# Where the fourth operand sum of layer 0's MLP is subtracted on VectorE

## The chip, the core and the metric

The kernel runs on one core of one Trainium2 chip. TensorE (PE) multiplies, with weight loads (PEld) that overlap its matmuls; VectorE (DVE), ScalarE (ACT) and GpSimd (POOL) do elementwise work; SyncE (SP) and ACT issue most DMAs. The metric is the time of one execution on the device, in microseconds (us).

## The reference

A two-layer encoder over two sequences (`x_prompt` and `x_sample`, each 512 tokens of width 1024, float32). Layer 0 mixes by a grouped Fourier transform, layer 1 by attention; each is followed by a squared-ReLU MLP of width 4096. The change lies in the MLP of layer 0:

```python
def rms_norm(x, g):
    x32 = x.astype(jnp.float32)
    y = x32 * lax.rsqrt(jnp.mean(x32 * x32, axis=-1, keepdims=True) + EPS)
    return (y * g.astype(jnp.float32)).astype(x.dtype)

def sq_relu_mlp(h, w_up, w_down):
    a = jnp.maximum(h @ w_up, 0)
    return (a * a) @ w_down

def trunk(x, ...):
    for i in range(DEPTH):
        j = i // N_MIXERS
        if i % N_MIXERS == 0:
            x = x + fourier_mix(rms_norm(x, fourier_norm[j]), fourier_w_out[j])
        else:
            x = x + gqa_attention(...)
        x = x + sq_relu_mlp(rms_norm(x, mlp_norm[i]), mlp_w_up[i], mlp_w_down[i])
    return rms_norm(x, final_norm)
```

## The kernel before, in words

**Precision.** A float32 product is made of three matmuls. Each operand is split into a high half (float32r, a cast on ACT, L82) and a low half (operand minus high half, a subtraction on DVE, L83); `product` (L863 on, matmul at L869) does high times high, high times low and low times high, accumulated in one PSUM bank. Over four blocks of depth, that is 12 matmuls of 128x128 by 128x512.

**The MLP's product in seven.** The up-projection of both sequences together is a 2x2 block product, and the kernel does it with seven block products instead of eight. The blocks are: sequence 0 or 1 on one side, and the lower or upper half of the model width on the other. The operands on the activations' side are two blocks of sequence 0 ("b11", "b21"), one block of sequence 1 ("b22") and four sums ("t1" to "t4"). With f[0] and f[1] the normed activations of the two sequences, c in (0, 1) a half of each operand:

- t1 = f[1, c] - f[0, c] (L266)
- t2 = f[1, 2+c] - t1 (L267)
- t3 = f[1, 2+c] - f[1, c] (L271), in place of f[1, c]
- t4 = f[0, 2+c] - t2 (L278), in place of f[0, 2+c]

Each half is a 128x1024 tile. `put` splits it into two new tiles of 128x1024 (high and low). All such tiles, the activations and the outputs of a pair come from one pool of 38 buffers ("u" in the trace, `slot` in the code); raw weights come from a pool of 5 ("raw"), split weights from one of 4 ("w").

**Order of the work around the change.** The class `Blocks` makes the operands. In layer 0 the generator `second_sums` makes those that need sequence 1, a step at each `yield`: for each half the norm of two blocks (L208), t1, t2 and t2's split; then t3 and its split; t1's split; t4 and its split; b22's split. `first_product` runs it while PE does the products that need sequence 0 alone. A pair p (16 in layer 0) is two tiles of 128 hidden units. `Pair.first` is the product with b11, copied out of PSUM by ACT at L903; `Pair.second` adds the product with b21 in the same bank, and ACT makes its squared ReLU (L884, L885). Pairs 0 to 7 do both of these ahead of the sums. In the loop over p = 0 to 7, PE does pair p's first product and pair p-1's second, the next pair's row weights are loaded and split, and then, from p = 3 on, three steps of `second_sums` are taken. Steps 1 to 3 (norms, t1 and t2 of c = 0) fall in p = 3, those of c = 1 in p = 4, t3 and the first t1 split in p = 5, the second t1 split and both t4 in p = 6, and b22 in p = 7. The sums of pair 0's own weights are made in between (`sums_13` at L918 and L919, `sum_2` at L922, `sum_4` at L930).

After the loop, `Pair.rest` does the products with t2, t3, t1, t4 and b22 for each pair, adds them up on DVE (L947 to L981), and makes, in the same turn, the weight sums of the next pair. Pairs 8 to 15 do their first and second products within it.

**Who sets the order.** The framework's scheduler orders each engine's instructions, by their place in the source and by when it takes their inputs to be ready; in the blocks under `manual_schedule` the named engines keep an order written out by hand. In the loop over p = 0 to 7 that holds for PE's products alone; the steps of `second_sums`, DVE, ACT and SP are the scheduler's. A buffer is given out again when the last reader of its old tile has run.

```python
            if p > 3 - whole:
                for _ in range(3 - 2 * l):
                    next(todo, None)
```

Of the kernel before, what the change touches and what calls it, by code (L numbers as in the profile page):

```python
# [40 lines left out]
def trunk_kernel(ctx, tc, x_in, xt_in, y_out, dcos, dsin, feat, rope, gfour, gcol, grow, gfin,  # L41
                 w_four, w_nyq, w_qkv, w_o, w_up, w_row2, w_row4, w_sum2, w_sum4, w_down):
    nc = tc.nc
# [17 lines left out]
    def slot(shape, dt):  # L61
        return act.tile(shape, dt, tag="u4", name=nm("u"))
# [122 lines left out]
    class Blocks:  # L185
# [70 lines left out]
        def second_sums(self):  # L256

            f, t1, t2 = self.f, [], []
            for c in range(2):
                self.norm(1, c)  # L260
                yield
                self.norm(1, 2 + c)
                yield
                t1.append(slot([P, 2, 512], F32))
                t2.append(slot([P, 2, 512], F32))
                nc.vector.tensor_sub(t1[c], f[1, c], f[0, c])  # L266
                nc.vector.tensor_sub(t2[c], f[1, 2 + c], t1[c])  # L267
                self.put("t2", t2[c])
                yield
            for c in range(2):  # L270
                nc.vector.tensor_sub(f[1, c], f[1, 2 + c], f[1, c])  # L271
                self.put("t3", f[1, c])
                yield
            for c in range(2):
                self.put("t1", t1[c])
                yield
            for c in range(2):
                nc.vector.tensor_sub(f[0, 2 + c], f[0, 2 + c], t2[c])  # L278
                self.put("t4", f[0, 2 + c])
                yield  # L280
            for c in range(2, 4):
                self.put("b22", f[1, c])
                yield
# [1672 lines left out]
```

## Time and profile before

| | us |
|---|---|
| median of 3 runs | 1694.37 |
| lowest, highest | 1693.82, 1695.23 |
| the profiled execution | 1695.11 |
| its span | 1693.3 |
| PE busy in the span | 1681.2 |
| DVE, ACT busy | 1228.0, 854.3 |
| mean granted TensorE clock | 0.999 |

The profile is of one execution. A row of a timeline gives the start in us from the span's start, the length in us, the engine, the line in the kernel, the operation, what is written and read (by the program's names without numbers) with its shape, and how many of them follow each other; in brackets stands how long the engine had been idle, and who ended that. A row of waits gives who waited for whom, the total in us, how often, and the longest. A row of a stretch gives its length, and busy us with the number of instructions for PE, PEld, DVE, ACT and POOL in turn, then the granted clock, the DMAs' busy share and GB/s. Matmuls are pipelined and their ends are modelled, so PE's busy time contains the overlap of neighbours.

### The profile page before, as it was taken

How to read it: one execution, taken by the hardware profiler on the slowest of the kernel's cores; microseconds unless marked ns; L12 is line 12 of the kernel's file. 1: busy time of each engine (PE TensorE's matmuls, PEld its weight loads, DVE VectorE, ACT ScalarE, POOL GpSimd, SP SyncE). 2: the span in 40 equal slices, each digit the busy share in tenths (PEclk: the TensorE clock that was granted, in tenths of full speed). 3: DMA queues.
4: the chain of work that ended last, by engine and by line, in shares of the span. 5: the costliest groups of instructions: out<-in, count | busy, mean ns of one | idle time of the engine just before them, and what ended most of it. 6: DMA issues, size and time to landing. Idle time of an engine off the chain costs nothing. (4 is left out here: it accounts for less than half of the span.)

```text
span 1693.3 us, 21857 instructions
## 1 busy us (share of the span) xinstructions
PE 1681.2 (99%) x7845; PEld 1395.0 (82%) x7845; DVE 1228.0 (73%) x1808; ACT 854.3 (50%) x1489; POOL 334.9 (20%) x304
## 2 busy tenths in 40 slices
PE   9999999999999999999999999999999999999998
PEld 7987888888888888888888888888888888888887
DVE  8778776557887879876588744687655479787864
ACT  7566444446243434457787714654444544344334
POOL 1321443221000000132344303014422200000002
PEclk9999999999999999999999999999999999999999
DMA  9643555449554644610000213335544686455322
GB/s 340 167 137 126 198 187 180 156 168 388 178 209 140 224 139 172 223 50 33 26 26 1 100 61 126 110 120 193 180 143 156 224 303 236 159 210 183 133 75 100
DMA packets 103679, 265.81 MB, mean 157 GB/s; under 512 B 10177, under 2 KB 10177, under 8 KB 103570
## 3 DMA queue, kind: packets, MB, share of 16 engines
q1 hardware_dynamic: 87266, 232.43, 39.2%
q10 hardware_dynamic: 14400, 26.22, 4.1%
q0 software_dynamic: 1904, 5.77, 1.7%
q8 instruction: 61, 1.00, 0.2%
q14 instruction: 48, 0.39, 0.1%
HBM read 189.40 MB, written 73.92 MB: 156 GB/s over the span
## 5 line engine op out<-in xcount | busy, mean ns | idle before, releaser
L869 PE MATMUL ps<-u,w 128*128 128x512 f32 x4656 | 1065.4, 389 | 1.4 <-ACT u L903 0.7
L869 PEld LDWEIGHTS ps<-u,w 128*128 128x128 f32 x4656 | 872.7, 188 | 185.6 <-ACT u L903 2.7
L82 ACT CAST w<-raw 128x1024 fp32r<-128x1024 f32 (+1 forms) x224 | 217.5, 981 | 445.1 <-PE ps L869 244.5
L83 DVE TENSOR_TENSOR w<-raw,w 128x1024 fp32r<-128x1024 f32 (+1 forms) x224 | 255.6, 1144 | 60.8 <-ACT w L82 60.3
L156 POOL TENSOR_TENSOR t<-t,t 128x512 f32<-128x512 f32 (+1 forms) x56 | 77.7, 1388 | 738.3 <-ACT t L154 682.2
L82 ACT CAST u<-u 128x1024 fp32r<-128x1024 f32 (+1 forms) x131 | 131.3, 1044 | 76.0 <-PE ps L869 47.2
L83 DVE TENSOR_TENSOR u<-u,u 128x1024 fp32r<-128x1024 f32 (+1 forms) x131 | 155.3, 1211 | 19.3 <-ACT u L82 18.6
L77 PE MATMUL ps<-u,u 128*128 128x512 f32 (+2 forms) x388 | 150.2, 388 | 0.4 <-DVE u L83 0.4
L1141 DVE TENSOR_TENSOR u<-ps,u 128x512 f32<-128x512 f32 x160 | 109.4, 686 | 51.2 <-PE ps L869 48.9
L78 PE MATMUL ps<-u,u 128*128 128x512 f32 (+2 forms) x388 | 144.4, 372 | 0.4 <-DVE u L83 0.3
L79 PE MATMUL ps<-u,u 128*128 128x512 f32 (+2 forms) x388 | 144.4, 372 | 0.0
L869 PE MATMUL ps<-u,u 128*128 128x512 f32 x576 | 137.8, 390 | 0.2 <-DVE u L1141 0.2
L869 PEld LDWEIGHTS ps<-u,u 128*128 128x128 f32 x576 | 107.9, 188 | 23.8 <-DVE u L1141 0.6
L989 POOL TENSOR_TENSOR u<-u 128x512 f32<-128x512 f32 x28 | 37.2, 1329 | 398.7 <-ACT u L885 398.7
L83 DVE TENSOR_TENSOR u<-ps,u 128x512 fp32r<-128x512 f32 (+4 forms) x118 | 74.7, 649 | 19.3 <-ACT u L82 18.3
L79 PEld LDWEIGHTS ps<-u,u 128*128 128x128 f32 x388 | 73.1, 188 | 12.9
L78 PEld LDWEIGHTS ps<-u,u 128*128 128x128 f32 x388 | 73.4, 189 | 11.7 <-DVE u L83 1.3
L77 PEld LDWEIGHTS ps<-u,u 128*128 128x128 f32 x388 | 73.3, 189 | 10.7 <-DVE u L83 0.6
L82 ACT CAST u<-ps 128x512 fp32r<-128x512 f32 (+4 forms) x118 | 65.5, 562 | 26.5 <-PE ps L79 11.5
L947 DVE TENSOR_TENSOR t<-ps,u 128x512 f32<-128x512 f32 x30 | 20.7, 690 | 80.0 <-PE ps L869 57.9
L852 DVE TENSOR_TENSOR u<-ps,u 128x512 f32<-128x512 f32 (+1 forms) x48 | 30.9, 644 | 64.4 <-PE ps L79 64.4
L77 PE MATMUL ps<-u,w 128*128 128x512 f32 (+2 forms) x192 | 65.0, 338 | 0.0
(247 smaller groups left out, 1983.8 us busy)
## 6 DMA issues: line engine op xcount, KB each, us to landing
raw<-w_up SPq DMA_DIRECT2D x82, 512.0 KB, 4.5
u<-spill_t SPq DMA_DIRECT2D x60, 512.0 KB, 6.1
raw<-w_sum SPq DMA_DIRECT2D x56, 512.0 KB, 4.2
u<-spill_b SPq DMA_DIRECT2D x45, 512.0 KB, 5.6
spill_t<-u SPq DMA_DIRECT2D x87, 256.0 KB, 2.0
spill_b<-t ACTq DMA_DIRECT2D x60, 256.0 KB, 3.4
raw<-w_row SPq DMA_DIRECT2D x28, 512.0 KB, 4.0
park<-u SPq DMA_DIRECT2D x24, 512.0 KB, 3.7
```

The source lines that it names most:

```text
L77: nc.tensor.matmul(out, lh, rh, start=first, stop=False)
L78: nc.tensor.matmul(out, lh, rl, start=False, stop=False)
L79: nc.tensor.matmul(out, ll, rh, start=False, stop=last)
L82: nc.scalar.copy(dst_hi, src)
L83: eng.tensor_sub(dst_lo, src, f32(dst_hi))
L156: nc.gpsimd.tensor_add(acc[q][:, :n], acc[q][:, :n], s[:, :n])
L852: nc.vector.tensor_add(x[:, :n], o[:, :n], x[:, :n])
L869: nc.tensor.matmul(o, w[x][:, sl], h[k][y], start=first and k + i == 0, stop=k == n - 1 and i == 2, skip_group_check=not first)
L947: nc.vector.tensor_add(u2, ob, t[:, 0])
L989: eng.tensor_sub(t[:, 0], b12, b11)
L1141: nc.vector.tensor_add(x, o, x)
```

## The change

The subtraction that makes t4 moves, for each half, from t4's own step to the end of the step that makes t2, behind t2's split. The split of t4 stays where it was. Nothing else changes; the function `second`, which layer 1 uses, keeps its order.

```diff
@@ -266,6 +266,7 @@
                 nc.vector.tensor_sub(t1[c], f[1, c], f[0, c])
                 nc.vector.tensor_sub(t2[c], f[1, 2 + c], t1[c])
                 self.put("t2", t2[c])
+                nc.vector.tensor_sub(f[0, 2 + c], f[0, 2 + c], t2[c])
                 yield
             for c in range(2):
                 nc.vector.tensor_sub(f[1, c], f[1, 2 + c], f[1, c])
@@ -275,7 +276,6 @@
                 self.put("t1", t1[c])
                 yield
             for c in range(2):
-                nc.vector.tensor_sub(f[0, 2 + c], f[0, 2 + c], t2[c])
                 self.put("t4", f[0, 2 + c])
                 yield
             for c in range(2, 4):
```

## Prediction

> **What bounds the kernel now.** I read the page first, then the waits of TensorE over the whole span, then the busy time in stretches around the edit, then the timelines of VectorE, ScalarE and TensorE there.
>
> ```profile
> span 1693.3 us, 21857 instructions
> ...
> PE 1681.2 (99%) x7845; PEld 1395.0 (82%) x7845; DVE 1228.0 (73%) x1808; ACT 854.3 (50%) x1489; POOL 334.9 (20%) x304
> ```
>
> TensorE (PE) is busy for 1681.2 of 1693.3 us. The change moves two VectorE (DVE) instructions and touches no matmul, so it can only change PE's waits. Their list, longest first, in us, times and longest one:
>
> ```profile
> PE ps L356 <- POOL u L334: 1.8, 1, 1.8
> PE ps L869 <- ACT u L903: 0.7, 1, 0.7
> PE ps L869 <- DVE w L83: 0.5, 1, 0.5
> ...
> PE ps L455 <- DVE t L429: 0.2, 1, 0.2
> ```
>
> The view has 13 rows from 1.8 down to 0.2, which sum to 5.6 us; the first belongs to the Fourier stage at the start. The second, 0.7 us, is the one inside the stretch that the change edits. There, in columns of length, then busy us and count for each engine:
>
> ```profile
> 121.40:134.50 13.10, 13.01 (x58) 10.43 (x57) 13.10 (x14) 9.31 (x12) 0.00 (x0) 1.00 0.35 120
> 134.50:138.00 3.50, 3.47 (x16) 2.54 (x14) 3.50 (x5) 3.02 (x4) 0.00 (x0) 1.00 0.40 144
> 138.00:148.00 10.00, 9.34 (x41) 7.74 (x42) 10.00 (x10) 8.57 (x12) 0.00 (x0) 1.00 0.28 96
> ```
>
> The third pair of numbers is DVE: 13.10 of 13.10, 3.50 of 3.50, 10.00 of 10.00. DVE is full here, with no slack to hide a moved instruction, while PE loses almost nothing. So the question is which of DVE's results PE, or ScalarE (ACT) on PE's behalf, waits for in these 27 us.
>
> **The change part by part.** Step 1, the work moved. Two subtractions of 128x1024 leave turn p=6 of the row loop and enter its turns p=3 and p=4, behind the second sum's split of each half. They issue no DMA, and their count is unchanged.
>
> ```profile
> 119.09 1.22 DVE L83 TENSOR_TENSOR w<-raw,w 128x1024 fp32r<-128x1024 f32 x1
> 120.22 1.21 DVE L267 TENSOR_TENSOR u<-u,u 128x1024 f32<-128x1024 f32 x1
> 121.36 2.35 DVE L208 TENSOR_TENSOR u<-u,t 128x1024 f32<-128x1024 f32 x2
> ...
> 125.90 1.21 DVE L83 TENSOR_TENSOR w<-raw,w 128x1024 fp32r<-128x1024 f32 x1
> 127.04 1.21 DVE L267 TENSOR_TENSOR u<-u,u 128x1024 f32<-128x1024 f32 x1
> 128.17 2.35 DVE L271 TENSOR_TENSOR u<-u,u 128x1024 f32<-128x1024 f32 x2
> ...
> 131.58 0.68 DVE L922 TENSOR_TENSOR raw<-raw,raw 128x512 f32<-128x512 f32 x1
> 132.18 1.21 DVE L83 TENSOR_TENSOR w<-raw,w 128x1024 fp32r<-128x1024 f32 x1
> ...
> 134.46 1.21 DVE L278 TENSOR_TENSOR u<-u,u 128x1024 f32<-128x1024 f32 x1
> 135.59 1.21 DVE L83 TENSOR_TENSOR u<-u,u 128x1024 fp32r<-128x1024 f32 x1
> 136.73 1.21 DVE L278 TENSOR_TENSOR u<-u,u 128x1024 f32<-128x1024 f32 x1
> 137.86 1.21 DVE L83 TENSOR_TENSOR u<-u,u 128x1024 fp32r<-128x1024 f32 x1
> ```
>
> From one L278 to its successor is 135.59 - 134.46 = 1.13 us. VectorE's order is the scheduler's, not the source's alone, but the moved instruction needs only L267's result, and now stands ahead of the norms of the next half (L208) in the source. So I expect the first at 121.36, directly after the first L267, and the second directly after the second L267. Then what DVE does between 121.36 and 128.25 comes 1.13 us later, what it does from 128.17 to 134.46 comes 2.27 us later, and after 137.86 it is where it was. DVE's total is the same.
>
> Step 2, a small extra. Each subtraction now reads what the instruction directly ahead of it wrote. The nearest rows with such an own wait and without one:
>
> ```profile
> 114.34 0.69 DVE L918 TENSOR_TENSOR raw<-raw,raw 128x512 f32<-128x512 f32 x1
> 115.07 0.69 DVE L919 TENSOR_TENSOR raw<-raw 128x512 f32<-128x512 f32 x1
> ...
> 144.67 0.68 DVE L930 TENSOR_TENSOR t<-raw,raw 128x512 f32<-128x512 f32 x1
> 145.28 2.35 DVE L83 TENSOR_TENSOR u<-u,u 128x1024 fp32r<-128x1024 f32 x2
> ```
>
> L919 overwrites what L918 reads and starts 0.73 us after it; L83 starts 0.61 us after an L930 of the same size that it doesn't depend on. So a wait on the predecessor costs 0.12 us by these rows, and 0.24 us for both, which makes the delay 2.5 us instead of 2.27. The end below is zero, if the scheduler sets another instruction between. I take 2.27, since the split's low half may well stand between.
>
> The Trainium skill's "VectorE: DVE Perf Modes", section "The DRAIN you can't avoid", says that a semaphore between chained VectorE operations costs nothing extra, because the pipeline empties after each anyway. By it the delay would stay 2.27 us. This trace disagrees by the 0.12 us above.
>
> Step 3, who waits for the delayed results. ACT casts the high half of every sum, and works in its compiled order:
>
> ```profile
> 124.50 1.06 ACT L82 CAST w<-raw 128x1024 fp32r<-128x1024 f32 x1
> 128.28 1.05 ACT L82 CAST u<-u 128x1024 fp32r<-128x1024 f32 x1 [2.73 <-DVE u L267]
> ...
> 130.89 0.59 ACT L903 COPY u<-ps 128x512 f32<-128x512 f32 x1 [0.40 <-ACT u L885]
> ...
> 132.33 1.05 ACT L82 CAST w<-raw 128x1024 fp32r<-128x1024 f32 x1
> 133.27 1.05 ACT L82 CAST u<-u 128x1024 fp32r<-128x1024 f32 x1
> 134.61 0.60 ACT L884 ACTIVATE u<-ps 128x512 f32<-128x512 f32 x1 [0.29 <-PE ps L869]
> ...
> 138.02 0.59 ACT L903 COPY u<-ps 128x512 f32<-128x512 f32 x1 [0.40 <-ACT u L885]
> ```
>
> At 128.28 ACT has stood idle for 2.73 us until the second L267. Behind that cast are queued the squares of a finished row product (L884, L885) and the copy L903 at 130.89. L903 saves a pair's first row product, and PE may add the second product into the same bank only after it:
>
> ```profile
> 131.53 6.01 PEld L869 LDWEIGHTS ps<-u,w 128*128 128x128 f32 x27 [0.51 <-ACT u L903]
> 138.66 15.08 PEld L869 LDWEIGHTS ps<-u,w 128*128 128x128 f32 x67 [1.11 <-ACT u L903]
> ```
>
> PE's weight loads start 0.05 us after the copies end, at 131.53 and 138.66, after idling 0.51 and 1.11 us. So PE has no margin against ACT here, and ACT none against DVE at 128.28. That is the only exposed chain. If ACT keeps its order, the first copy and PE slip by 1.13 us. The cast at 132.33 starts when L922 (131.58 + 0.68 = 132.26) ends, which is then 134.53: 2.27 us later. The 0.29 us that ACT spends waiting for PE at 134.61 take up a part, so the copy at 138.02, and PE at 138.66, come 2.27 - 0.29 = 1.98 us later. The first slip is contained in it. Upper end: +1.98 us, or +2.2 with step 2.
>
> Lower end. The scheduler makes ACT's order anew. With the cast of L267's result known to be later, it can put the squares and the copy ahead of it; both products they read are finished by then. The idle time at 131.53 can go, and so can that at 138.66, at most 0.51 + 1.11 = 1.62 us.
>
> Step 4, the weights' low halves. PE does 12 matmuls for a product:
>
> ```profile
> 108.49 5.71 PE L869 MATMUL ps<-u,w 128*128 128x512 f32 x24
> 114.04 0.60 PE L170 MATMUL ps<-ident,s 128*128 128x128 f32 x4
> 114.39 23.57 PE L869 MATMUL ps<-u,w 128*128 128x512 f32 x101
> ```
>
> 24 take 114.04 - 108.49 = 5.55 us, 2.78 a product. From 114.39 five products come before pair 6's first, so it starts at about 128.3; its low half (125.90 + 1.21 = 127.11) becomes 128.24, still in time. Pair 7's (132.18 + 1.21 = 133.39) becomes 135.66; it is needed after the product that starts at 131.53, so at 134.31, or 135.44 with PE's own slip: 0.2 us late, inside the 1.98. The sums' later uses are far off. SP's loads wait for buffers that these splits free, so each may issue up to 2.27 us later; GpSimd does nothing here.
>
> ```profile
> 120.33 25.91 SPq L91 DMA_DIRECT2D raw<-w_up x5
> ```
>
> TensorE's list of waits names no load, so I put 0; if that cover were gone, the cost is at most the 2.27 us.
>
> Step 5, the gain side of the edit. The fourth sum is ready 13 and 8 us earlier, and with it the buffer of each second sum (two of 38) is free that much earlier. Neither has a waiter in the trace: L278's results are cast between other casts with ACT busy all the while, and no PE wait is on them. Worth 0 unless the scheduler uses it (rival below).
>
> The sum. Ends -1.62 and +1.98 us in the stretch. The likeliest is a mixed order: the squares go ahead of the late cast, which takes back the 0.51, and L922's 2.27 us are felt in part at 138. The middle of the ends is +0.2; the row nearest to my case is the cast idle 2.73 us for DVE, which speaks for the upper half, so I take +0.4 us. The profiled execution took 1695.11 us (span 1693.3 and 1.8 around it) and would become 1695.5; it lies 0.74 above the median of the runs, 1694.37. From the median: 1694.37 + 0.4 = 1694.8 us. A measurement of this kernel can tell about 0.2%, 3.4 us, from no change.
>
> **The rivals.**
> *ACT keeps its order.* For: the 2.73 us show that its order takes no account of DVE's real lateness. Time: 1694.37 + 1.98 = 1696.3 us. Chance 0.19.
> *Slower, in the later pairs.* The scheduler lays out everything behind the edit anew. The place is pairs 8 to 15, whose first product is copied by L903 in the running loop.
>
> ```profile
> PEld ps L869 <- ACT u L903: 2.7, 6, 1.1
> ```
>
> Of 6 waits and 2.7 us, 1.62 are the two above, so 1.1 us in four small waits are left for all other pairs. If the re-laid order set this copy behind another cast in each of eight pairs, at 0.51 each it costs 4.1 us, at 1.11 it costs 8.9: 1698.5 us and up. It decides from 3.4/8 = 0.43 us a pair. Against: buffers and turns are the same there. Chance 0.16.
> *Buffers come free earlier and both pauses go.* 1694.37 - 1.62 = 1692.8 us. Against: TensorE names ACT's copy, not a buffer. Chance 0.07. With more of the other waits gone it could pass 3.4 us; they sum to 5.6 - 1.8 - 0.7 = 3.1, and with the 1.62 it would need over half of them: 0.05.
> The Trainium skill's "Perfetto Trace Analysis", section "Identifying Performance Opportunities", says that a repeated gap on the engine that should be full can mean that there is too little SBUF for the next tile; that is this rival, and two gaps in 1693 us are hardly its pattern.
> *Nothing moves.* The scheduler places the subtractions where they were: 1694.4 us. Against: they are ready early and now come first. Chance 0.08.
>
> **How the numbers follow.** Mixed order 0.45, ACT's order kept 0.19, later pairs 0.16, pauses gone 0.07, more than that 0.05, nothing 0.08. Faster by over 0.2%: 0.05. Slower by over 0.2%: 0.16. Within: 0.79. The range goes from the pauses gone, 1692.8, less 0.2 for what the median moves, to the lower end of the later pairs, 1698.5: 1692.6 to 1698.5; what it leaves out is the 0.05 and most of the 0.16.
>
> **What would show it.** L278's new line should appear once or twice between 121 and 131 us with 1.2 us each, DVE should be full up to 148 us, and the two L267 should lie about 1.13 and the L271 2.27 us apart from before. PE's wait for L903 tells forecast (under 1.6 us in the stretch), ACT's order kept (2.5 to 3), and pauses gone (none) apart. Step 3 is wrong if the casts of L267's results come later and PE's waits don't follow; the whole is wrong if the time moves by over 3.4 us, and then the waits behind 160 us must show it.

## The result and the profile after

The changed kernel takes 1699.97 us (median of 7 runs, 1699.18 to 1700.48) beside 1694.58 us for the kernel before (7 runs, 1693.82 to 1695.23). The ratio is 1.0031, with a 95% interval of 1.0021 to 1.0040: slower by 5.4 us, more than the 0.2% that a measurement can tell. The profiled execution has a span of 1698.2 us.

The page of the kernel after, busy us of each engine:

```profile
PE 1683.5 (99%) x7845; PEld 1397.5 (82%) x7845; DVE 1228.0 (72%) x1808; ACT 854.2 (50%) x1489; POOL 334.2 (20%) x304
```

The work is the same, instruction for instruction. PE's busy time has grown by 2.3 us all the same, with the same count of matmuls: some of them must have run longer. The longest of TensorE's waits over the span of the kernel after:

```profile
PE ps L869 <- DVE w L83: 4.3, 2, 3.8
```

ACT's copy L903 has left the list, and the low half of a weight (L83), 0.5 us before, heads it with 4.3 us, of which one wait is 3.8 us. TensorE's timeline of the kernel after puts that wait in its place:

```profile
114.58 19.77 PE L869 MATMUL ps<-u,w 128*128 128x512 f32 x86
138.18 21.61 PE L869 MATMUL ps<-u,w 128*128 128x512 f32 x82 [3.83 <-DVE w L83]
159.62 2.88 PE L869 MATMUL ps<-u,u 128*128 128x512 f32 x12
```

And the two rows of the kernel before that stand behind the 101 matmuls of the row at 114.39:

```profile
138.66 15.50 PE L869 MATMUL ps<-u,w 128*128 128x512 f32 x67 [0.69 <-ACT u L903]
154.00 2.88 PE L869 MATMUL ps<-u,u 128*128 128x512 f32 x12
```

Both run 168 matmuls from the same point to the first product of operands only (`u,u`): 154.00 - 114.39 = 39.61 us before, 159.62 - 114.58 = 45.04 after. So 5.43 us are lost here. Behind it nothing more is lost or won up to 390 us. Each pair has such a product; that of pair 14, before and then after:

```profile
387.99 2.88 PE L869 MATMUL ps<-u,u 128*128 128x512 f32 x12
```

```profile
393.64 2.88 PE L869 MATMUL ps<-u,u 128*128 128x512 f32 x12
```

From the one to the other it is 233.99 us before and 234.02 after. All pairs from 8 to 15 run in the same time.

The pause itself is 3.83 us. The rest is in the granted clock (the sixth figure behind the engines' pairs, ahead of the DMA share). Stretches of the kernel after:

```profile
134.30:137.20 2.90, 0.05 (x1) 0.00 (x0) 2.90 (x4) 2.87 (x5) 0.00 (x0) 1.00 0.00 0
137.20:140.60 3.40, 2.42 (x6) 1.95 (x7) 3.40 (x4) 3.40 (x6) 0.00 (x0) 0.50 0.58 201
140.60:144.00 3.40, 3.40 (x10) 2.63 (x9) 3.40 (x4) 1.90 (x3) 0.00 (x0) 0.50 0.08 30
144.00:147.40 3.40, 3.40 (x17) 2.80 (x16) 1.54 (x2) 1.18 (x3) 0.00 (x0) 0.99 0.24 45
```

TensorE stands still from 134.35. At 137.2, while it still does, its clock falls to 0.50, and it stays there for 6.8 us. In 140.60 to 144.00 TensorE is busy all the time and starts 10 matmuls; in the stretch of the same length behind, 17. What this costs is read from the 82 matmuls behind the pause: 159.62 - 138.18 = 21.44 us here, 18.72 us in an experiment below in which the same 82 run at full clock. That is 2.72 us. So the 5.43 us come out as 3.83 (pause) + 2.72 (clock) - 1.26 (the pauses of the kernel before, which are gone) = 5.29, with 0.14 left over. The 1.26 are 39.61 less 168 matmuls at 18.72/82 = 0.228 us.

Why the low half comes so late is seen in VectorE's timeline of the kernel after, one row an instruction; the L83 of `w` in it is pair 7's:

```profile
122.68 1.22 DVE L269 TENSOR_TENSOR u<-u,u 128x1024 f32<-128x1024 f32 x1
...
129.49 1.21 DVE L272 TENSOR_TENSOR u<-u,u 128x1024 f32<-128x1024 f32 x1
130.63 1.22 DVE L269 TENSOR_TENSOR u<-u,u 128x1024 f32<-128x1024 f32 x1
131.76 1.21 DVE L83 TENSOR_TENSOR u<-u,u 128x1024 fp32r<-128x1024 f32 x1
132.90 1.22 DVE L272 TENSOR_TENSOR u<-u,u 128x1024 f32<-128x1024 f32 x1
134.03 1.21 DVE L83 TENSOR_TENSOR u<-u,u 128x1024 fp32r<-128x1024 f32 x1
135.17 0.68 DVE L922 TENSOR_TENSOR raw<-raw,raw 128x512 f32<-128x512 f32 x1
135.77 1.22 DVE L83 TENSOR_TENSOR u<-u,u 128x1024 fp32r<-128x1024 f32 x1
136.91 1.22 DVE L83 TENSOR_TENSOR w<-raw,w 128x1024 fp32r<-128x1024 f32 x1
```

The rows of the kernel before that the prediction leaves out are VectorE's two L83 of operands around the row, and ScalarE's cast of the first half of t3:

```profile
130.44 1.21 DVE L83 TENSOR_TENSOR u<-u,u 128x1024 fp32r<-128x1024 f32 x1
...
133.32 1.21 DVE L83 TENSOR_TENSOR u<-u,u 128x1024 fp32r<-128x1024 f32 x1
```

```profile
131.38 1.05 ACT L82 CAST u<-u 128x1024 fp32r<-128x1024 f32 x1
```

Pair 7's low half starts at 136.91, where before it started at 132.18: 4.73 us later. 0.19 of it is this execution's lag at 114.4 us (114.58 against 114.39). The other 4.54 are four instructions of 1.135 us: the two moved L269, and two low halves of operands (t3's, by the buffer numbers) that now stand ahead of the row's; before, one L83 of `u`, t2's second, lay between the L271 and L922, and now three lie ahead of the row. So the order was not kept. The row's split belongs to pair 7 and is written in the turn p = 6; t3's split is written in p = 5. By their place in the source t3's halves go first. In the kernel before, the cast of t3's first half ended at 132.43, just behind the start of the row's half, and the row came first; 2.27 us later that cast is made (at 132.12 after), and t3's half goes first. For the second half (cast ended at 135.19) the profile doesn't show this, and how the scheduler reckoned is not on record: the order itself is shown, its reason is argued. TensorE does the first two matmuls of pair 7's product with the high half, then pair 5's second product (by the buffer numbers), and then needs the low half at 134.35; it ends at 138.12. The source has these two matmuls behind pair 5's second product, so TensorE's order in the loop is not wholly the written one either.

### The profile page after: what moved, and what is told of

The parts are those of the page before. It is cut to its first block, busy times and chain, and to the rows that moved or that the text cites. A ratio compares the mean times of both kernels' runs of the same rounds, so it can differ in the third digit from the quotient of the medians.

```text
span 1698.2 us, 21857 instructions
## 1 busy us (share of the span) xinstructions
PE 1683.5 (99%) x7845; PEld 1397.5 (82%) x7845; DVE 1228.0 (72%) x1808; ACT 854.2 (50%) x1489; POOL 334.2 (20%) x304
## 5 line engine op out<-in xcount | busy, mean ns | idle before, releaser
L83 DVE TENSOR_TENSOR w<-raw,w 128x1024 fp32r<-128x1024 f32 (+1 forms) x224 | 255.5, 1143 | 60.0 <-ACT w L82 59.5
L83 DVE TENSOR_TENSOR u<-u,u 128x1024 fp32r<-128x1024 f32 (+1 forms) x131 | 155.4, 1211 | 23.0 <-ACT u L82 22.3
L83 DVE TENSOR_TENSOR u<-ps,u 128x512 fp32r<-128x512 f32 (+4 forms) x118 | 74.7, 649 | 19.3 <-ACT u L82 18.2
```

The lines of the kernel that those rows point to most:

```text
L83: eng.tensor_sub(dst_lo, src, f32(dst_hi))
```

## The experiments

**Theories.** *Order*: it is VectorE's 2.27 us of work ahead of the row, plus the two halves that overtake it, plus the clock that a long pause brings down; the operation and its buffers don't matter. Rivals: *buffers or readiness* (the fourth sum being ready early, or the second sum's buffer being free early, re-lays something else); *work alone* (each subtraction costs its share wherever it is); and for the clock, that its fall has another cause than the pause.

The table has each kernel's median with its range and runs, the kernel before beside it on the same chip, the ratio, and two lengths from the profiled execution: the stretch from the first of the 168 matmuls to the `u,u` product (39.61 us before, 45.04 after), and the lowest granted clock in it. The profile is of one execution: for the extra work once and for GpSimd it was the slowest of those timed, for the change with the row first and for the first run of 6 fillers the fastest.

| kernel | us | before | ratio, 95% interval | stretch | clock |
|---|---|---|---|---|---|
| first half alone moved | 1696.91 (1695.76-1698.23, 10) | 1694.76 | 1.0013 (1.0004-1.0022) | 40.51 | 1.00 |
| second half alone moved | 1696.39 (1695.77-1698.09, 10) | 1694.76 | 1.0011 (1.0001-1.0021) | 40.52 | 1.00 |
| before with extra work | 1699.86 (1698.67-1701.71, 6) | 1694.76 | 1.0031 (1.0019-1.0043) | 45.00 | 0.50 |
| change, row first | 1697.44 (1696.36-1698.82, 10) | 1694.76 | 1.0015 (1.0006-1.0024) | 41.09 | 1.00 |
| change, 17 fillers | 1698.27 (1697.01-1699.65, 11) | 1694.88 | 1.0019 (1.0010-1.0028) | 42.36 | 1.00 |
| change on GpSimd | 1699.56 (1698.79-1701.16, 7) | 1694.88 | 1.0029 (1.0018-1.0040) | 44.66 | 0.50 |
| before, row first | 1693.87 (1693.51-1694.51, 11) | 1694.88 | 0.9993 (0.9984-1.0002) | 39.28 | 1.00 |
| before, extra work twice | 1700.81 (1700.38-1701.49, 5) | 1694.88 | 1.0036 (1.0023-1.0048) | 46.15 | 0.50 |
| change, row and sums first | 1694.35 (1693.41-1695.54, 11) | 1695.06 | 0.9996 (0.9987-1.0005) | 39.35 | 1.00 |
| change, 6 fillers | 1698.62 (1696.52-1699.80, 11) | 1695.06 | 1.0019 (1.0010-1.0028) | 42.32 | 1.00 |
| the same once more | 1698.61 (1) | 1695.00 | - | 43.77 | 0.50 |
| change, 3 fillers | 1699.93 (1697.53-1702.97, 8) | 1695.00 | 1.0031 (1.0021-1.0042) | 43.67 | 0.50 |

### One half of the change at a time

For the first half; the second has `c == 1`:

```diff
+                if c == 0:
                     nc.vector.tensor_sub(f[0, 2 + c], f[0, 2 + c], t2[c])
...
             for c in range(2):
+                if c != 0:
+                    nc.vector.tensor_sub(f[0, 2 + c], f[0, 2 + c], t2[c])
                 self.put("t4", f[0, 2 + c])
```

> Only the first half's subtraction moves; the second half's stays in t4's own step. Order theory: VectorE is 1.13 us late and pair 7's low half also falls behind the low halves of both t3, so it ends 1.13 us earlier than in the changed kernel, at about 137.0 us; TensorE is ready for it at 134.35, so one pause of 2.65 us. If the clock falls only after a pause of more than about 3 us, the granted clock stays 1.00 and the time is the kernel before less its two small pauses (1.1) plus 2.65: about 1.6 us over before, 1696.2. If a pause of any length gives a slow stretch in proportion (2.8 us for 3.83), it is 2 us more: 1698.2. Delay-only theory (no re-ranking, 1.13 us): no pause, as before. Buffer theory (the earlier free buffer of t2 is the cause): about half of the change's loss, 1697.3.

> Only the second half's subtraction moves. Order theory: again one subtraction and both t3 low halves stand ahead of pair 7's low half, so the same pause of about 2.65 us and the same time as with the first half alone, 1696.2 with a clock that holds, 1698.2 with one that falls in proportion. Delay-only theory: no pause, as before. Buffer theory: less than the first half alone, since this buffer comes free only some 9 us earlier instead of 13.

Measured 1696.91 and 1696.39 us: 2.2 and 1.6 us above before, and each at less than half of the whole change's 5.4. VectorE's timeline with the first half alone moved:

```profile
133.44 2.35 DVE L83 TENSOR_TENSOR u<-u,u 128x1024 fp32r<-128x1024 f32 x2
135.71 1.22 DVE L83 TENSOR_TENSOR w<-raw,w 128x1024 fp32r<-128x1024 f32 x1
```

One subtraction alone makes the row's half 135.71 - 132.18 = 3.53 us late, and three instructions of 1.135 us are 3.41: one moved, and both of t3's halves, which pass the row already. TensorE in the same kernel:

```profile
134.66 1.21 PE L872 MATMUL ps<-u,w 128*128 128x512 f32 x4 [0.37 <-ACT w L82]
136.99 18.20 PE L872 MATMUL ps<-u,w 128*128 128x512 f32 x78 [1.11 <-DVE w L83]
155.03 2.88 PE L872 MATMUL ps<-u,u 128*128 128x512 f32 x12
```

Here TensorE's own order, too, is another: four matmuls of the sums' products stand between pair 5's second product and the rest of pair 7's (by the buffer numbers). So the pause comes in two parts of 0.37 and 1.11 us, where one of 2.65 was expected, and the clock stays. The stretch is 40.51 us, 0.9 longer than before. Twice that is 1.8, not 5.4: the two halves together cost a jump more. The 0.9 us lie inside the 95% intervals of the two ratios (from 0.7 and 0.2 us up); the medians are above it by 1.2 and 0.7 us, which these runs leave open.

### Extra work in the kernel before, and twice as much

```diff
                 self.put("t2", t2[c])
+                nc.vector.tensor_sub(t1[c], f[1, c], f[0, c])
```

The kernel before with t1 computed again, same value, at the place of the moved instruction; the second version computes it twice over. The fourth sum stays where it was.

> The kernel before, with t1 computed a second time (same inputs, same value) behind t2's split of each half: the same VectorE work at the place where the change puts its subtractions, but t4 stays in its own step, t2's buffers live as long as before, and nothing is ready earlier. Order theory: pair 7's low half stands behind the same instructions as in the changed kernel, so the same pause of 3.8 us and the same slow clock behind it: about 1700 us. Buffer theory, and any theory in which t4's earlier readiness matters: as before, 1694.6 us, as VectorE's 2.3 us of extra work would be felt only at a wait that the theory does not name.

> The kernel before, in its own order, with the first sum of each half computed twice over behind the second sum's split: four extra subtractions on VectorE, 4.5 us of work that changes no value. Theory (pause = lateness of pair 7's low half; a pause over some 3 us brings a stretch of half clock of fixed length): the low half comes some 5 to 6 us later than in the kernel before, the pause is about 5 to 6 us, the slow stretch again about 6 us long (2.8 us lost): 1701 to 1702.5 us. Rival (the loss from the clock grows with the pause): 14 matmuls become some 20, 1703 us or more. Rival (the time goes with VectorE's added work alone, 2.27 us for 5.2 us as one extra subtraction per half gave): 1705 us.

Measured 1699.86 us, as the change. TensorE's timeline with the work once:

```profile
138.29 21.56 PE L870 MATMUL ps<-u,w 128*128 128x512 f32 x82 [3.83 <-DVE w L83]
```

The same pause to a hundredth, with none of the early readiness and none of the freed buffers. That ends the rival *buffers or readiness*: 2.27 us of other work at this place do the same. With twice the work it takes 1700.81 us, 0.95 more, just under what the theory had. The row's half starts at 138.22 us, 1.31 later than after; but TensorE comes to it later too, so that its pause is 3.99 us, where 5 to 6 were expected. Stretches of that kernel:

```profile
138.40:141.80 3.40, 2.30 (x6) 1.82 (x6) 3.40 (x4) 3.40 (x5) 0.00 (x0) 0.50 0.32 89
141.80:145.20 3.40, 3.40 (x9) 2.63 (x8) 3.40 (x4) 2.21 (x3) 0.00 (x0) 0.50 0.16 66
```

Again 6.8 us at half clock. *Work alone* would have added another 5 us for them; it is out as well.

### The change with the row ranked first, and with the next gate too

```diff
-                        pairs[p + 1].split_row()
+                        with tc.high_priority(40) if p + 1 == ah - 1 else nullcontext():
+                            pairs[p + 1].split_row()
```

No instruction is added or removed; the split of pair 7's row is ranked 40 places earlier.

> The changed kernel, with pair 7's row split ranked ahead of the t3 step for the scheduler (nothing else in the source). Order theory: its low half then stands behind the two subtractions alone, 2.27 us later than before, ends at about 134.1 and TensorE, ready at 134.35, does not wait for it: the 3.8 us wait for VectorE is gone. What comes next is ACT's copy of pair 6's first product, which in this order stands behind four casts of which one waits for the second t3 and one for L922: it may end as late as 140.9 while TensorE wants it at about 137.2, which would be a pause of up to 3.7 us and a slow clock again, up to 1699.5; if these casts are earlier, down to 1694. Buffer theory: no change against the changed kernel, the wait stays.

Measured 1697.44 us, about half of the loss back. TensorE's timeline:

```profile
138.91 1.21 PE L869 MATMUL ps<-u,w 128*128 128x512 f32 x4 [1.74 <-ACT w L82]
140.55 15.72 PE L869 MATMUL ps<-u,w 128*128 128x512 f32 x68 [0.43 <-DVE w L83]
```

The wait for the row is gone from this place. The next in line shows: the cast and the low half of the weights' second sum, which needs L922 (started at 131.58 before, at 136.75 here). The expectation had named the copy of pair 6's first product as the next. Pauses of 2.2 us, and the clock stays at 1.00 in this execution; whether it fell in slower ones is not seen. So the second version ranks that gate ahead as well:

```diff
-                pairs[0].sums_23()
+                with tc.high_priority(40):
+                    pairs[0].sums_23()
             if 2 * np_ == NF and p == 6:
-                pairs[0].split_23()
+                with tc.high_priority(40):
+                    pairs[0].split_23()
```

> The changed kernel with two groups of steps ranked 40 places earlier, no instruction more or less: the split of pair 7's row, and the second sum and the two splits of the first pair's sum weights (the next gate that the kernel with the row first showed). Planned order on VectorE: the row's low half at seat 184, some 11 instructions behind the first L267 at 120.4 us, that is at about 132.4 us, where the kernel before has it (132.18). Theory (the whole loss is the order that the two moved subtractions bring about): no pause over 1 us between 130 and 142 us, clock 1.00, the u,u product near 154.0 to 154.7 us, time 1694.3 to 1695.3 us. Rival (the 2.27 us of earlier work on a full VectorE must come out somewhere): a further gate opens, the u,u product at 155.5 us or later, 1696 to 1697.5 us.

Measured 1694.35 us, ratio 0.9996 (0.9987 to 1.0005): the two moved subtractions are still at their new place, and the loss is gone. VectorE's timeline here, the last row being pair 7's half:

```profile
129.90 1.22 DVE L269 TENSOR_TENSOR u<-u,u 128x1024 f32<-128x1024 f32 x1
...
132.17 1.22 DVE L83 TENSOR_TENSOR w<-raw,w 128x1024 fp32r<-128x1024 f32 x1
```

The row's half is back at 132.17 (132.18 before), and TensorE's timeline has one pause, of 0.87 us, in front of an earlier row:

```profile
130.03 23.87 PE L869 MATMUL ps<-u,w 128*128 128x512 f32 x104 [0.87 <-DVE w L83]
153.74 2.88 PE L869 MATMUL ps<-u,u 128*128 128x512 f32 x12
```

With the order put right nothing of the loss is left, within the interval. (Both rankings together were not tried on the kernel before, so what they are worth there is open; the first alone follows.) The rival, that 2.27 us on a full VectorE must come out somewhere, is wrong here: what is pushed back (t3's halves) has no one waiting.

### The same ranking in the kernel before

The first diff above, on the kernel before.

> The kernel before, with the split of pair 7's row ranked 40 places earlier and nothing else. Theory (TensorE's pauses of 0.25 and 0.85 us before 135 us in the kernel before come from the copies of pair 6's product behind casts on ScalarE, and the row's low half has some slack): one cast fewer ahead of the copy, about 0.9 us less: 1693.7 us. Rival (ranking the row ahead only pushes the sums' halves behind it, which the next product then waits for, as in the changed kernel with the row first): a wait of 1 to 2 us at 137 to 141 us appears and the time is 1695 to 1696 us.

1693.87 us, ratio 0.9993 (0.9984 to 1.0002). The stretch is 39.28 us, 0.33 shorter than before, where 0.9 was expected; of the pauses of the weight loads (PEld) the one of 0.51 us at L903 stays. No gain can be told from none. Nor does any other run give a version that beats the kernel before by more than its interval.

### The moved subtractions on GpSimd

```diff
-                nc.vector.tensor_sub(f[0, 2 + c], f[0, 2 + c], t2[c])
+                nc.gpsimd.tensor_sub(f[0, 2 + c], f[0, 2 + c], t2[c])
```

> The changed kernel with the two moved subtractions on GpSimd in place of VectorE. Theory (order on VectorE decides: without the two subtractions and their 2.27 us, pair 7's low half is ready in time as in the kernel before): no pause over 1 us between 130 and 140 us, clock 1.00, and the time of the kernel before, 1694.0 to 1694.8 us. Rival (the early readiness of the fourth sums itself lets their casts and low halves go ahead of pair 7's row, whoever computes them): their low halves still stand before the row's, at least 2.2 us late, and the time is 1696 to 1697 us. A third way: VectorE's instructions beside GpSimd's get slower, as beside the copies, and part of the 2.27 us is lost again: 1695 to 1696 us.

1699.56 us: all three expectations missed. The part about order holds, as the row's half starts at 133.05 us and no wait of TensorE names it. But GpSimd's timeline, two instructions in one row:

```profile
122.40 23.69 POOL L269 TENSOR_TENSOR u<-u,u 128x1024 f32<-128x1024 f32 x2 [14.02 <-DVE u L267]
```

The first of them took 20.41 us, the second 3.32, where VectorE takes 1.22. VectorE's instructions kept their 1.23 us and stood without a gap up to 140.47; only then did three of them take 7.96. The Trainium skill's "SBUF — State Buffer" says in its list of terms that these two engines share a pair of ports which one holds for a whole instruction while the other stands blocked; a GpSimd instruction that waits among VectorE's without end agrees with that, though no run here separates ports from other causes. The fourth sums' casts stand early in ACT's queue, and the copy L903 behind them. ACT's timeline:

```profile
146.12 1.04 ACT L82 CAST u<-u 128x1024 fp32r<-128x1024 f32 x1 [2.23 <-POOL u L269]
...
147.56 0.58 ACT L903 COPY u<-ps 128x512 f32<-128x512 f32 x1
```

And TensorE, 0.05 us behind that copy:

```profile
148.19 11.91 PE L869 MATMUL ps<-u,w 128*128 128x512 f32 x44 [4.13 <-ACT u L903]
159.94 2.88 PE L869 MATMUL ps<-u,u 128*128 128x512 f32 x12
```

A pause of 4.13 us from another queue and at another time. Its 44 matmuls take 159.94 - 148.19 = 11.75 us instead of 44 x 0.228 = 10.03: the clock has fallen here too, so its fall goes with the pause and not with VectorE's order.

### Filling the pause

```diff
+                if whole and p == ah - 1:
+                    o, x, y = ps(), blocks.b["b11"][0][0], blocks.b["b21"][0][0]
+                    for _ in range(17):
+                        nc.tensor.matmul(o, x[:, 0, :P], y[:, 0], start=True, stop=True)
                 pair.first()
```

The changed kernel with 17, 6 or 3 extra matmuls whose result nobody reads. They run ahead of the wait, so that TensorE stands still for less of it, and the row is ready no sooner.

> The changed kernel with 17 extra matmuls (finished high halves of two other blocks, result read by nobody) set ahead of pair 7's first product, so that TensorE has some 17 x 0.227 = 3.9 us of work where it stood still for 3.83 us. Theory (a pause of 3.83 us makes the granted clock fall to 0.50 for some 6 us, which costs 2.8 us by itself): the pause nearly goes, the clock stays 1.00 behind it, and the time falls by about 2.8 us to some 1697.2 us, though the kernel has more work than the changed one. Rival (the clock falls for another reason than the pause, or only the late half of the row counts): the slow stretch stays and the time is that of the changed kernel, 1699.5 to 1700.5 us.

With 17 the pause is gone, the clock stays at 1.00, and the stretch is 42.36 us, of which 17 x 0.228 = 3.88 are the extra matmuls: 2.7 us less than after, with more work. The time, 1698.27 us, is 1.7 under the change: between the theory's 1697.2 and the rival's 1699.5, though the profile has no slow stretch at all. The 1.1 us above the theory stay open.

> The changed kernel with 6 extra matmuls (result read by nobody) ahead of pair 7's first product in place of 17. Theory (the length of the pause decides over the clock): TensorE's pause before pair 7's product shrinks from 3.83 to about 2.4 us, the clock holds 1.00 as it did over 2.5 us of pauses, and the time is that of the kernel with 17, about 1697 to 1698.3 us. Rival (a pause over 2 us in one piece is enough): a stretch at clock 0.50 follows, and the time is 1699 to 1700 us.

> The kernel with 6 extra matmuls once more, for its profile: its eleven times fell into two groups, four of 1696.5 to 1697.5 us at mean clocks of 0.999 to 1.000 and seven of 1698.6 to 1699.8 us at 0.998 to 0.999, and the profile is of the first. Theory (a pause of 2.5 us is on the border: whether the clock falls hangs on where the pause lies in windows of some 3.4 us in which the clock is set, so it falls in some executions): if this execution is of the second group, its profile shows some 3.4 us at clock 0.50 behind the pause, 1.5 to 1.7 us lost, and nothing else new; if of the first, 1.00 throughout. Rival (the two groups come from the later parts of the kernel): the second group's profile has 1.00 from 134 to 150 us and the time lost elsewhere.

The same kernel twice. TensorE's timeline, first execution:

```profile
138.03 18.89 PE L869 MATMUL ps<-u,w 128*128 128x512 f32 x82 [2.47 <-DVE w L83]
156.75 2.88 PE L869 MATMUL ps<-u,u 128*128 128x512 f32 x12
```

And the second one's:

```profile
138.12 20.34 PE L869 MATMUL ps<-u,w 128*128 128x512 f32 x82 [2.47 <-DVE w L83]
158.29 2.88 PE L869 MATMUL ps<-u,u 128*128 128x512 f32 x12
```

The pause is 2.47 us in both and at the same place, and the 82 matmuls take 18.72 and 20.17 us. The stretches of the second execution tell why:

```profile
137.80:141.20 3.40, 3.08 (x7) 2.48 (x8) 3.40 (x4) 3.40 (x5) 0.00 (x0) 0.50 0.51 160
141.20:144.60 3.40, 3.40 (x16) 2.76 (x15) 3.40 (x4) 1.25 (x2) 0.00 (x0) 0.99 0.00 0
```

The clock is at 0.50 for 3.4 us, half as long as after, and this costs 20.17 - 18.72 = 1.45 us. In the first execution the stretch from 137.80 to 141.20 has 1.00. So with 6 fillers the time of an execution hangs on whether the clock fell: of the eleven timed ones four took 1696.5 to 1697.5 us and seven 1698.6 to 1699.8, and the median, 1698.62, falls between the two expectations. That each of these seven had a fall is worked out from the times, from the lower mean clock of five of them and from the one profile, not seen in each. Why one execution had it and the other not is answered below, by where the pause lies.

> The changed kernel with 3 extra matmuls: a pause of about 3.83 - 3 x 0.227 = 3.15 us. Theory of the windows: the clock falls in most executions, for one window of 3.4 us or two, so times of 1698.5 to 1700 us, a median near 1699.2. Rival (a fixed bound of about 3 us on the pause): as the changed kernel in every execution, 1699.2 to 1700.5 us, median 1699.9.

The pause is 3.15 us as worked out, and the profile has 3.4 us at half clock (82 matmuls in 20.07 us). The median, 1699.93, is the rival's and the range of 1697.53 to 1702.97 wider than either had: by the times this run doesn't tell the two apart. A bound fixed at about 3 us is refuted all the same, by the second execution with 2.47 us.

## Why the prediction was wrong

*The result*, +5.4 us, lies outside 1692.6 to 1698.5 and in the case given 0.16.

*Step 1* held for the work (two instructions of 1.22 us ahead of the row, 2.27 us) and failed for the order. The subtractions stand one place later than forecast, behind L208 and L272 (122.68 and 130.63). What did the harm is the sentence that follows from it, that everything in between just comes 1.13 or 2.27 us later. The scheduler ranked the queue anew, and two instructions that stood behind the row passed it.

*Step 2* was not put to the test: another instruction (L208 at 121.54, L272 at 129.49) stands between each L267 and its L269, the case for which the prediction had zero. The choice of 2.27 was right.

*Step 3* was right in part. ScalarE's timeline of the kernel after (the cast is that of the second L267, the copies are pair 5's and pair 6's, by the buffer numbers):

```profile
129.66 1.03 ACT L82 CAST u<-u 128x1024 fp32r<-128x1024 f32 x1
130.60 0.58 ACT L903 COPY u<-ps 128x512 f32<-128x512 f32 x1
...
138.14 0.58 ACT L903 COPY u<-ps 128x512 f32<-128x512 f32 x1
```

The scheduler did put the squares (128.49 and 129.12) ahead of the late cast. The copy still stands behind it, but ends at 131.18 in place of 131.48, and the first wait for L903 is gone, as the lower end had it. The second is gone for another reason. Pair 6's copy ends at 138.72 (138.61 before), but TensorE, held by pair 7's low half, asks for it only ten matmuls behind 138.18. With the low half in time it would have asked at about 134.35 + 10 x 0.228 = 136.6 and waited some 2.1 us, an estimate that is near the prediction's upper end; the change with the row first has 2.2 us of pauses behind the same product. So a longer wait covered this one. The prediction's 0.51 and 1.11 are idle times of the weight loads; TensorE's own excess in the kernel before is the 1.26 us above. And it was wrong that this is "the only exposed chain".

*Step 4 is the step that failed*, on the order that step 1 took as kept: pair 7's low half, "needed" at 134.31 and ready at 135.66, "0.2 us late, inside the 1.98". TensorE needed it at 134.35, as worked out; it was ready at 138.12, 2.46 later than forecast, of which 2 x 1.135 are t3's two halves. The slip by which the prediction excused the first part of the lateness (135.44) was the very wait that step 3 had going away, so the two steps used different cases. And the pause had a price that no term of the sum contained, the 2.72 us at half clock.

*Step 5* was right: the freed buffers and the early sums are worth nothing; the run with extra work has the same time without them.

*The rivals.* "Slower, in the later pairs" had the sign and the wrong place: 233.99 and 234.02 us for what lies behind. "Pauses gone" saw both waits for L903 gone, the second for another reason, and had the time wrong by its sign. The telling signs were set on L903 and on waits behind 160 us; the loss is at 134 to 144 us, in L83.

*The clock.* The Trainium skill's "TensorE: Matmul & The Clock Gate", section "What's actually happening", says that the clock is set to half or full by how busy TensorE was in free-running windows of some 3.4 us, and its table under "Why this matters for your kernels" warns of idle gaps over about 3 us. The windows and the half rate agree with every fall seen here (0.50, for 3.4 or 6.8 us). The bound of 3 us is not tight by these runs: 2.47 us was enough in one execution of two. With the row 1.35 us late (135.66 against 134.31), no fall was to be expected from that bound; with the 3.77 us that it was late (138.12 against 134.35), one was.

## What to carry to other kernels

Moving work ahead on a full engine is not a shift of what lies behind: ask, for each instruction that feeds the bounding engine, which neighbours become ready within the delay and pass it, and price it with them. If a pause of the matrix engine comes to over 2 us, reckon with a stretch at half clock behind it, 1.4 to 2.7 us here; 2.47 us brought it in one execution and not in another. When a move costs by order alone, rank the instruction that is waited for, and the next gate behind it, instead of undoing the move.

## What the runs showed of the hardware

The granted clock falls on a grid. Each fall in the stretch lasted 3.41 us (GpSimd, 6 fillers, 3 fillers) or twice that, 6.83 us (after, extra work once and twice). At the end of the kernel, where TensorE's work thins out (1.83 us in the last 8.2 of the kernel after), the clock falls once more, and in all six executions the two falls begin a whole number of lengths of 6.827/2 = 3.413 us apart: after, (1697.10 - 137.21) / 3.413 = 457.0; the others 457, 456, 453, 456 and 456. So the windows run on through the execution, and are not started by a pause.

By this grid the two executions with 6 fillers can be told apart. In the second, the fall starts at 137.83, and the window ahead of it holds 1.24 us of work:

```profile
134.41:137.83 3.42, 1.24 (x6) 0.70 (x4) 3.42 (x4) 3.39 (x5) 0.00 (x0) 1.00 0.19 74
```

In the first, the fall at the end (1693.48) puts window edges at 133.59 and 137.00, so that the same pause lies in two windows, with 1.97 and 2.38 us of work. The first of them:

```profile
133.59:137.00 3.41, 1.97 (x9) 1.31 (x7) 3.41 (x5) 2.97 (x4) 0.00 (x0) 1.00 0.00 0
```

In the kernel after, the fall came 2.85 us after TensorE stopped (134.35 to 137.20) and lasted two windows; with 4.13 us of pause (on GpSimd) it lasted only one, and began when TensorE was working again:

```profile
142.40:145.80 3.40, 1.66 (x8) 1.04 (x6) 3.36 (x2) 1.05 (x1) 3.40 (x2) 1.00 0.67 259
145.80:149.20 3.40, 1.01 (x4) 0.86 (x5) 3.37 (x4) 3.08 (x5) 0.29 (x1) 1.00 0.00 0
149.20:152.60 3.40, 3.40 (x9) 2.63 (x8) 3.39 (x4) 1.35 (x2) 0.00 (x0) 0.51 0.20 77
```

So a longer pause can cost less clock than a shorter one (1.7 us here, 2.72 after), by where it lies in the windows. A window busy for 1.66 of 3.40 us kept the clock, and one busy for 1.24 (6 fillers, second execution) or 1.01 lost it; at half clock one busy for 2.42 (after) did not bring it back, and one busy for 3.08 (6 fillers) did. A GpSimd subtraction of 128x1024 beside a full VectorE took 20.41 us.
